# Feed forward as 2x2 blocks with seven multiplications, with the down part's right-hand blocks summed in the gate and up part and kept in DRAM

## The chip, the cores and the metric

The kernel runs on one core of one Trainium2 chip. The metric is the device time of one execution in microseconds; lower is better. The kernel before takes 1798.79 us, the median of 3 runs between 1797.85 and 1799.35.

## The reference

One layer of a decoder for one inference step: 1024 prompt tokens and 8 sample tokens (one each of 8 sequences with 2048 cached positions), 1024 channels, 8 heads, 2816 feed forward channels, all in fp32. What matters here is the end of the layer, cut from the reference:

```python
D_MODEL = 1024; SEQ = 1024; DEC_BATCH = 8; D_FF = 2816; N_HEADS = 8; D_V = 64

def _layer(x, c, pos, attend, ...):
    mod = jax.nn.silu(c) @ w_ada + b_ada
    sh1, sc1, gt1, sh2, sc2, gt2 = jnp.split(mod[:, None, :], 6, axis=-1)
    h = _rmsnorm(x, g_norm1) * (1 + sc1) + sh1
    ...
    o = attend(q_nope, q_pe, c_kv, k_pe)
    a = jnp.einsum("bshd,hde->bse", o, w_attn_o)
    ...
    m = jax.nn.sigmoid(gate_a) * a + jax.nn.sigmoid(gate_b) * bb
    x = x + gt1 * (m @ w_out)
    h2 = _rmsnorm(x, g_norm2) * (1 + sc2) + sh2
    gg, up = jnp.split(h2 @ w_gu, 2, axis=-1)
    x = x + gt2 * ((jax.nn.silu(gg) * up) @ w_down)
    return x, c_kv, k_pe, u_ext[:, -POOL_STATE:]
```

## The kernel before

Activations stand with channels on the 128 partitions and the T = 1032 tokens (8 sample tokens first, then the prompt) along the free axis. Each fp32 operand of a large product is split into a high and a low fp32r part: `split` (lines 97 and 106) makes the high part on ScalarE and the low part, source minus high part, on VectorE or GpSimd. `_mm3` (lines 71 to 73) then issues three matmuls for each 128 x 128 weight tile: high by high, high by low, low by high.

The layer runs in stages. First the input projection and the norms of queries, keys and values. Then the sample tokens' attention over the cached pages (`decode`) and the prompt's attention by heads (`attention`), between which a generator of fillers stands: projections of the gates and of the pooling branch, and `ada_unit` (line 142), which makes 128 of the 6144 gate coefficients `mod`. Units 16 to 47 are fillers. `back` follows. It loads the heads' outputs from DRAM, multiplies six of eight heads with `w_attn_o` while the last heads still run (`pm`, `wo_hi`, `wo_lo`; result in `part`), adds the last two heads' part (`rest`, with `wlh`, `wll`), applies the gates (`mt`, lines 1035 and 1044), multiplies with `w_out`, adds the residual (`gated_add`, line 999), sums squares by matmul (`st2`), and makes the second norm (`rstd2`, lines 1113 and 1114; multiply, line 1119). All this goes over three chunks of C3 = 344 tokens, and the weights of `w_out`, once split, stay in SBUF for all three.

`feed_forward` works in four parts of 6, 6, 5 and 5 tiles of 128 feed forward channels. A part makes gate and up for each of its tiles, eight k tiles in each of three chunks; silu, the product with up (line 1167) and the split follow. Then for each of the eight output tiles it multiplies the part's activations with `w_down` and adds the result to x1, which stays in SBUF. Weights come through `wload` (line 1138): a DMA from SyncE's queue, a split, and a slot of a ring of four pairs.

```python
for wh, wl in ws:
    acc = ps.tile([P, 512], F32, name="pj", tag="mm")[:, :C3]
    for k in range(8):
        _mm3(nc, acc, wh[:, k], wl[:, k], h2[i][0][k], h2[i][1][k], k == 0, k == 7)
    accs.append(acc)
```

The order on each engine comes from a scheduler that takes the program's order as priority and moves an instruction ahead where its inputs and buffers are free; `_Urgent` marks some weights' loads as first. Buffers come from pools, where the tag names the buffer that a tile takes over, and a tile waits until its tag's last reader is done.

## Time and profile before

| | before |
|---|---|
| median of 3 runs | 1798.79 us |
| span of the profiled execution | 1798.7 us |
| TensorE busy (matmuls / weight loads) | 97% / 91% |
| VectorE, ScalarE, GpSimd busy | 46%, 34%, 17% |
| feed forward, 1047.0 to the end | 751.7 us |
| attention's last two heads, mixing and output projection, 833 to 1047 | 214 us |

A busy share is the time in which the engine ran an instruction, over the span. Matmuls overlap, so a matmul's duration is longer than the distance to the next one, and the work done is read from counts and from first and last starts. The granted clock of TensorE is given as a share of full speed.

### The profile page before, as it was taken

Reading aid. Unit: us, or ns where it says so; the run is one execution under the profiler, and the core shown is the slowest. Engines: PE = TensorE matmul, PEld = TensorE weight load, DVE = VectorE, ACT = ScalarE, POOL = GpSimd, SP = SyncE. Lnnn points to the kernel's source line nnn. Section 1 sums busy time; section 2 is a strip of 40 time slices with the busy share of each in tenths; the row PEclk is TensorE's granted clock in tenths of the full one; section 3 lists DMA queues with packets and bytes.
Section 4 is the critical chain, followed back from the end, with each engine's and each line's share of the span. In section 5 each row is a group of like instructions: output and inputs, shape, how many; then the busy total and the mean of one; then the engine's idle time right before and its main releaser. Section 6 shows DMA issues by size and latency. Waiting matters only on the chain.

```text
span 1798.7 us, 30723 instructions
## 1 busy us (share of the span) xinstructions
PE 1741.1 (97%) x11840; PEld 1641.8 (91%) x11840; DVE 828.8 (46%) x1731; ACT 614.2 (34%) x1521; POOL 307.2 (17%) x336
## 2 busy tenths in 40 slices
PE   6799999999999999999989999999999999999999
PEld 5799999789687899998889899999999999999999
DVE  5656665547332455555787852233222322242223
ACT  5433555546341355545542332211221112111210
POOL 2524201001011223222575630000000000000000
PEclk9899999999999999999999999999999999999999
DMA  9213635445636433335523211111111121111112
GB/s 376 63 58 105 209 99 151 147 131 158 186 101 204 157 124 125 124 122 179 158 86 97 70 42 53 36 48 60 47 42 36 53 59 39 30 62 47 39 57 82
DMA packets 112147, 182.70 MB, mean 102 GB/s; under 512 B 15193, under 2 KB 86770, under 8 KB 110978
## 3 DMA queue, kind: packets, MB, share of 16 engines
q1 hardware_dynamic: 112002, 180.75, 32.4%
q8 instruction: 93, 1.52, 0.4%
q14 instruction: 52, 0.43, 0.1%
HBM read 151.77 MB, written 28.93 MB: 100 GB/s over the span
## 4 chain that ended last, share of the span: by engine, by line
PE 80%; DMA 4%; DVE 4%; issue 2%; ACT 1%; POOL 1%; SPq 1%; DVEq 0%; ACTq 0%; POOLq 0%
PE pj L71 19%; PE pj L72 19%; PE pj L73 19%; PE kn L71 4%; PE kn L72 3%; PE kn L73 3%; PE dacc L958 2%; PE tpp L679 2%; PE ada_ps L142 1%; PE av L693 1%; PE av L694 1%; PE sc L71 1%; PE sc L73 1%; PE sc L72 1%; PE tp L628 1%
## 5 line engine op out<-in xcount | busy, mean ns | idle before, releaser
L73 PE MATMUL pj<-h2h,fw 128*128 128x344 f32 x1056 | 337.1, 319 | 0.0
L72 PE MATMUL pj<-h2l,fw 128*128 128x344 f32 x1056 | 336.9, 319 | 0.0
L71 PE MATMUL pj<-h2h,fw 128*128 128x344 f32 x1056 | 335.7, 319 | 0.0
L73 PEld LDWEIGHTS pj<-h2h,fw 128*128 128x128 f32 x1056 | 198.3, 188 | 0.0
L72 PEld LDWEIGHTS pj<-h2l,fw 128*128 128x128 f32 x1056 | 198.2, 188 | 0.0
L71 PEld LDWEIGHTS pj<-h2h,fw 128*128 128x128 f32 x1056 | 198.1, 188 | 0.0
L97 ACT ACTIVATE fw<-fraw 128x1024 fp32r<-128x1024 f32 (+2 forms) x76 | 72.0, 948 | 302.4 <-PE pj L72 302.4
L73 PE MATMUL pj<-acth,fw 128*128 128x344 f32 x528 | 169.0, 320 | 0.0
L72 PE MATMUL pj<-actl,fw 128*128 128x344 f32 x528 | 168.9, 320 | 0.0
L71 PE MATMUL pj<-acth,fw 128*128 128x344 f32 x528 | 168.6, 319 | 0.0
L71 PE MATMUL pj<-hh,wt_hi 128*128 128x344 f32 x480 | 159.8, 333 | 0.0
L1167 DVE TENSOR_TENSOR silu<-silu,pj 128x344 f32<-128x344 f32 x66 | 33.8, 512 | 270.7 <-PE pj L73 270.7
L72 PE MATMUL pj<-hl,wt_hi 128*128 128x344 f32 x480 | 157.5, 328 | 0.0
L73 PE MATMUL pj<-hh,wt_lo 128*128 128x344 f32 x480 | 157.4, 328 | 0.0
L71 PE MATMUL kn<-wuh,lh 128*128 128x256 f32 (+1 forms) x512 | 150.4, 294 | 1.9 <-ACT nr L903 1.0
L72 PE MATMUL kn<-wul,lh 128*128 128x256 f32 (+1 forms) x512 | 145.3, 284 | 0.0
L73 PE MATMUL kn<-wuh,ll 128*128 128x256 f32 (+1 forms) x512 | 144.9, 284 | 0.0
L902 ACT ACTIVATE dsq<-kn 128x256 f32<-128x256 f32 x256 | 95.1, 380 | 111.5 <-PE kn L73 103.5
L999 DVE SCALAR_TENSOR_TENSOR x<-pj,mod,x 128x344 f32<-128x344 f32 (+1 forms) x96 | 55.0, 573 | 149.9 <-PE pj L73 149.9
L106 DVE TENSOR_TENSOR fw<-fraw,fw 128x1024 fp32r<-128x1024 f32 (+2 forms) x76 | 83.5, 1099 | 76.5 <-ACT fw L97 74.5
L904 DVE TENSOR_REDUCE ssq<-dsq 128x8 f32<-128x512 f32 x128 | 86.7, 679 | 52.5 <-ACT dsq L902 52.0
L71 PEld LDWEIGHTS kn<-wuh,lh 128*128 128x128 f32 x512 | 96.6, 189 | 13.0 <-issue 5.7
(328 smaller groups left out, 3778.9 us busy)
## 6 DMA issues: line engine op xcount, KB each, us to landing
fraw<-wgu_t SPq DMA_DIRECT2D x44, 512.0 KB, 3.6
pg<-cpack SPq DMA_DIRECT2D x128, 144.0 KB, 2.4
ln<-cnat SPq DMA_DIRECT2D x128, 128.5 KB, 2.4
wraw<-wada_t SPq DMA_DIRECT2D x32, 512.0 KB, 3.9
wraw<-win_t SPq DMA_DIRECT2D x20, 512.0 KB, 4.2
nat_d<-nat SPq DMA_DIRECT2D x8, 1024.0 KB, 4.5
natr<-nat_d SPq DMA_DIRECT2D x8, 1024.0 KB, 5.2
fraw<-wdn_t SPq DMA_DIRECT2D x16, 384.0 KB, 3.2
```

What stands on the lines that cost most here:

```text
L71: nc.tensor.matmul(out, sh, mh, start=first, stop=False)
L72: nc.tensor.matmul(out, sh, ml, start=False, stop=False)
L73: nc.tensor.matmul(out, sl, mh, start=False, stop=last)
L97: nc.scalar.activation(dst, src, AF.Copy)
L106: e.tensor_tensor(dl, src, dh.bitcast(F32), op=ALU.subtract)
L142: nc.tensor.matmul(acc[32 * j:32 * j + 32, 0:P], self.sT[:, kt, :], w[:, kt], start=(kt < 4), stop=(kt >= 4), tile_position=(0, 32 * j))
L679: nc.tensor.transpose(tp[:, s, i * P:(i + 1) * P], pn[:, i, kb * P:(kb + 1) * P], self.ident)
L902: nc.scalar.activation(sq[:, half].rearrange("p h d -> p (h d)"), kn[:, o:o + 256], AF.Square)
L904: nc.vector.tensor_reduce(ssq[:, j, t], sq.rearrange("p a h d -> p (a h) d"), axis=AX.X, op=ALU.add)
L958: nc.tensor.matmul(acc[32 * j:32 * j + 8, :W], p[:, j, t], ln[:, j], start=(t == 0), stop=False, tile_position=(0, 32 * j))
L999: nc.vector.scalar_tensor_tensor(dst[:, s0:], acc[:, s0:], gt[:, j, 8:9], res[:, s0:], op0=ALU.mult, op1=ALU.add)
L1167: nc.vector.tensor_tensor(s, s, accs[1], op=ALU.mult)
```

## The change

The feed forward's two products are each cut into 2 x 2 blocks and made with seven block products instead of eight (Winograd's form). The token columns are the two halves of 516 (`T2`). Each half is in turn handled as two pieces of `HC` = 258 columns, so a "half" `i` of the program, 0 or 1, holds one piece of both column blocks.

Gate and up: the left matrix has gate and up as its block rows, even and odd k tiles as its block columns; the right matrix is h2. In each of the 22 steps, `weights` loads gate and up weights of one tile and `left` makes four sums of their blocks on GpSimd (`sums`), then splits all seven left blocks (`wst`, tags w0 to w6). The seven right blocks (`cmb`) of each half are made once, in `norm`: four are sums of h2 blocks (`tcm`, lines 1131 to 1134, on VectorE and GpSimd). A step's products run over both halves, 12 matmuls of 258 columns each; PSUM holds running sums, which ScalarE copies out between products (`p1`, `u2`, `u4`), VectorE adds, and GpSimd multiplies with silu of the gate.

Down: the left matrix is w_down with output tiles 0 to 3 and 4 to 7 as block rows, even and odd feed forward tiles as block columns; the right matrix is the activations. After each second step VectorE makes the four sums of right blocks and both halves' seven blocks go to DRAM (`stg`, `cmb_d`, line 1316). Steps 1 to 12 also load parts of w_down, sum them on GpSimd (`dsum`) and write them to DRAM (`ws_d`). After step 22 the seven products follow one after the other, each over 11 k tiles, four output tiles and two halves: right blocks are loaded (`cml`, line 1369) and split, left blocks loaded (line 1378) and split into three rotating pairs of buffers. A product is added to x1, which goes through DRAM in between (`x1_d`; loaded again as `xacc`, line 1338), in `add`; the last two adds of an output tile write it out.

To make this fit, `back` goes over two halves of 516 columns in place of three chunks. The output weights are loaded and split for each half. For the second half the part of six heads is kept (`six`) while the first half's mixing runs with all eight heads. Eight of the 32 filler units of gate coefficients, 40 to 47 (`gt2`, which only the down part needs), move into step 0 of the feed forward (`gate_late`).

Cut to the core (comments and the new mixing code left out; the new lines are those of the changed kernel):

```diff
-FPARTS = (6, 6, 5, 5)
+T2 = T // 2
+HC = T // 4
...
-        units = iter(range(16, 48))
+        units = iter(range(16, 40))
...
+            def norm(i, x1, st, cm, tiles):
+                rs = xw.tile([P, T2], F32, name="rstd2", bufs=1)
+                nc.scalar.activation(two(rs), st, AF.Sqrt, scale=1.0 / DM, bias=self.eps)
+                nc.vector.reciprocal(rs, rs)
+                yield
...
+                    nc.vector.tensor_tensor(x, x, rs, op=ALU.mult)
...
+                    nc.scalar.activation(x, x, AF.Identity, scale=self.a2[:, j, 8:9], bias=sh2[:, j, 8:9])
...
+                for o in range(2):
+                    for q in range(4):
+                        act(2 * q + o)
+                        put(o, q, x1[2 * q + o][:, n1])
+                        yield
+                tm = tiles(i)
+                for r2 in range(2):
+                    for q in range(2):
+                        b11, b21 = x1[4 * r2 + 2 * q], x1[4 * r2 + 2 * q + 1]
+                        t1, t2, t3, t4 = (z[:, q * HC:(q + 1) * HC] for z in tm[r2])
+                        nc.vector.tensor_tensor(t1, b11[:, n2], b11[:, n1], op=ALU.subtract)
+                        nc.gpsimd.tensor_tensor(t3, b21[:, n2], b11[:, n2], op=ALU.subtract)
...
+    def sums(self, s, a11, a12, a21, a22):
+        tt = self.nc.gpsimd.tensor_tensor
+        tt(s[0], a21, a22, op=ALU.add)
+        tt(s[1], s[0], a11, op=ALU.subtract)
+        tt(s[2], a11, a21, op=ALU.subtract)
+        tt(s[3], a12, s[1], op=ALU.subtract)
+    def left(self, a11, a12, a21, a22, n):
...
+        for o, src in enumerate((a11, a12, s[1], s[2], s[0], s[3], a22)):
+            w = self.W.tile([P, 8, P], F32R, name="wst", tag=f"w{o}")
+            self.split(w[:, 0:n], w[:, 4:4 + n], src, "a")
...
+            for f in range(NF):
+                if f:
+                    w = weights(f)
...
+                for i in range(2):
+                    b[i] = bank("fb")[:, :HC]
+                    run(b[i], 0, i)
+                    p1[i] = t("p1")
+                    nc.scalar.activation(p1[i], b[i], AF.Copy)
...
+                for i in range(2):
+                    run(b[i], 4, i, True)
+                    u4[i] = t("u4")
+                    nc.scalar.activation(u4[i], b[i], AF.Copy)
+                    nc.vector.tensor_tensor(u4[i], d[i], u4[i], op=ALU.add)
+                for i in range(2):
+                    run(b[i], 5, i, True)
+                    nc.scalar.activation(n2[i], b[i], AF.Silu)
+                    nc.gpsimd.tensor_tensor(n2[i], n2[i], u4[i], op=ALU.mult)
...
+                        nc.sync.dma_start(self.cmb_d[:, f // 2, :, i].rearrange("o p n -> p o n"), z)
+                if f == 0:
+                    for k in range(40, 48):
+                        self.gate_late(k, ev, bank)
+                elif units:
...
+                    self.sums([s[:, k, :n] for k in range(4)], raws[0][:, 0:n], raws[0][:, 4:4 + n], raws[1][:, 0:n],
+                              raws[1][:, 4:4 + n])
...
+            x = xp.tile([P, T], F32, name="xacc", tag=f"xa{j}")
+            nc.sync.dma_start(x, self.x1_d[j])
...
+        for n, (o, s, blk, dm, h, new, final) in enumerate((
+                (0, None, (0, 0), 0, 0, True, False), (2, 1, None, 4, 0, False, False), (4, 0, None, 4, 1, False, False),
+                (5, 3, None, 0, 1, False, True), (1, None, (0, 1), 0, 0, True, True), (3, 2, None, 4, 1, True, True),
+                (6, None, (1, 1), 4, 0, False, True))):
+            for q in range(NP):
+                z = self.sp.tile([P, T2], F32, name="cml", tag=f"s{q % 4}")
+                nc.sync.dma_start(two(z), self.cmb_d[o, q])
...
+                for p0, k in ((0, 6), (6, 5)):
+                    raw = self.fw.tile([P, 8, P], F32, name="fraw")[:, :k]
...
+                    hl = [self.W.tile([P, 8, P], F32R, name="wdn", tag=f"w{(2 * nw + z) % 6}")[:, :k] for z in range(2)]
```

VectorE at the last norm, before: the third chunk's root is inverted, then multiplies with it (line 1119) alternate with the low parts of h2 (line 106) and with the activations of the first feed forward tile (silu).

```order
L1114 RECIPROCAL rstd_13179<-rstd_13179 128x344
L1167 TENSOR_TENSOR silu<-silu,pj 128x344
L1119 TENSOR_TENSOR t_13182<-x_2_12890,rstd_13179 128x344
L1119 TENSOR_TENSOR t_13189<-x_2_12890,rstd_13179 128x344
L106 TENSOR_TENSOR actl<-silu,acth 128x344
L106 TENSOR_TENSOR h2l<-t_13182,h2h 128x344
L1119 TENSOR_TENSOR t_13196<-x_2_12890,rstd_13179 128x344
L106 TENSOR_TENSOR h2l<-t_13189,h2h 128x344
```

The same engine now, at the norm of the second half (rstd, line 1104; x1b is x1 of that half):

```order
L1104 RECIPROCAL rstd_13324<-rstd_13324 128x516
L1109 TENSOR_TENSOR x1b<-x1b,rstd_13324 128x516 x8
L1131 TENSOR_TENSOR tcm<-x1b 128x258 x2
L109 TENSOR_TENSOR cmb<-x1b,cmb 128x258
L1131 TENSOR_TENSOR tcm<-x1b 128x258
L109 TENSOR_TENSOR cmb<-x1b,cmb 128x258
L1131 TENSOR_TENSOR tcm<-x1b 128x258
L1133 TENSOR_TENSOR tcm<-x1b,tcm 128x258
L109 TENSOR_TENSOR cmb<-x1b,cmb 128x258
```

Eight multiplies of 516 columns now stand in a row behind the reciprocal, and the first low part that the feed forward needs (cmb) stands behind them and two differences.

TensorE where the feed forward begins, before: the last output projection matmuls (pj from mh and wout) and the first of gate (fw0, fw1: weight tile, high and low part).

```order
L72 MATMUL pj_13143<-ml_12816,wout0_12317 128x344
L73 MATMUL pj_13143<-mh_12815,wout1_12318 128x344
L71 MATMUL pj_13260<-h2h_12381,fw0_13248 128x344
L72 MATMUL pj_13260<-h2l_12382,fw0_13248 128x344
L73 MATMUL pj_13260<-h2h_12381,fw1_13249 128x344
L71 MATMUL pj_13260<-h2h_12390,fw0_13248 128x344
```

TensorE now, at the end of the first product's first half and behind it (fb and fa: sums of the first and second product; wst_13303 and wst_13306: their weights; cmb_13263 is of the second half, the other cmb are of the first):

```order
L1255 MATMUL fb_13421<-cmb_12574,wst_13303 128x258
L1256 MATMUL fb_13421<-cmb_12576,wst_13303 128x258
L1257 MATMUL fb_13421<-cmb_12574,wst_13303 128x258
L1255 MATMUL fb_13436<-cmb_13263,wst_13303 128x258
L1255 MATMUL fa_13451<-cmb_12577,wst_13306 128x258
L1256 MATMUL fa_13451<-cmb_12579,wst_13306 128x258
L1257 MATMUL fa_13451<-cmb_12577,wst_13306 128x258
```

The matmuls of one tile followed one another; now a single matmul of the second half stands between the first half's first product and its second, in the place where the second half's first right block comes in.

SyncE's queue where the last gate and up tiles end, before: the fourth part's loads of gate and up weights, of down weights, then the outputs.

```order
L1138 DMA fraw<-wgu_t 128x1024 x10
L1138 DMA fraw<-wdn_t 128x640 x8
L1138 DMA fraw<-wgu_t 128x1024 x10
L1138 DMA fraw<-wdn_t 128x640 x6
L1178 DMA o_yT<-x_0_11920 128x344
```

SyncE's queue now, at the border between the gate and up part and the down part (stg: the last pair's blocks; fraw: left blocks; xacc: x1 back from DRAM, x_d; cml: right blocks):

```order
L1369 DMA cml<-cmb_d 128x516 x6
L1378 DMA fraw<-wdn_t 128x768
L1369 DMA cml<-cmb_d 128x516 x2
L1316 DMA cmb_d<-stg 128x7x258 x2
L1378 DMA fraw<-wdn_t 128x640
L1338 DMA xacc<-x_d 128x1032 x8
L1369 DMA cml<-cmb_d 128x516
L1378 DMA fraw<-ws_d 128x768
```

The last blocks' write stands ahead of eight loads of x1, and the load that reads these blocks back (the one cml behind xacc) stands behind them. On TensorE, 108 matmuls of the down part stand between the last of the gate and up part and the first that reads this load.

## Rows read from the trace of the kernel before

**Rows 1.** The page: busy time of each engine; granted clock in 40 slices.

```profile
PE 1741.1 (97%) x11840; PEld 1641.8 (91%) x11840; DVE 828.8 (46%) x1731; ACT 614.2 (34%) x1521; POOL 307.2 (17%) x336
...
PEclk9899999999999999999999999999999999999999
```

**Rows 2.** Windows: us, then busy us (count) of PE, PEld, DVE, ACT, POOL; clock, DMA share, GB/s.

```profile
833.00:1047.00 214.00, 196.64 (x1229) 185.25 (x1222) 165.89 (x352) 94.89 (x220) 117.75 (x111) 0.98 0.40 119
835.30:873.90 38.60, 31.37 (x184) 26.22 (x183) 28.64 (x83) 22.84 (x64) 13.62 (x16) 0.96 0.93 283
873.90:917.00 43.10, 43.10 (x300) 42.12 (x299) 33.01 (x92) 22.83 (x63) 23.65 (x26) 1.00 0.23 72
917.00:1047.00 130.00, 119.87 (x721) 114.94 (x720) 103.29 (x176) 46.91 (x85) 80.15 (x70) 0.97 0.29 86
1047.00:1798.70 751.70, 748.19 (x4760) 747.90 (x4758) 217.87 (x383) 134.74 (x217) 7.91 (x9) 1.00 0.16 48
```

**Rows 3.** Matmuls and weight loads by form: busy us, mean ns of one, idle before.

```profile
L73 PE MATMUL pj<-h2h,fw 128*128 128x344 f32 x1056 | 337.1, 319 | 0.0
...
L73 PEld LDWEIGHTS pj<-h2h,fw 128*128 128x128 f32 x1056 | 198.3, 188 | 0.0
...
L73 PE MATMUL pj<-acth,fw 128*128 128x344 f32 x528 | 169.0, 320 | 0.0
...
L71 PE MATMUL pj<-mh,wout 128*128 128x344 f32 x192 | 62.0, 324 | 0.0
...
L71 PE MATMUL pm<-o,wo_hi 128*128 128x344 f32 x72 | 24.5, 341 | 2.1 <-ACT o L97 2.0
...
L71 PE MATMUL pm<-o,wlh 128*128 128x344 f32 x24 | 9.0, 376 | 5.0 <-DVE mt L1035 4.6
```

**Rows 4.** Feed forward: one line's matmuls with first and last start; the last matmul.

```profile
L71 PE MATMUL pj<-h2h,fw x1056: 313/318/324, 1047.4 to 1737.8; 128*128 128x344 f32 x176
...
1794.87 0.32 PE L73 MATMUL pj<-acth,fw 128*128 128x344 f32 x1
```

**Rows 5.** Timeline of TensorE, matmuls of 256 and 264 columns: start, duration.

```profile
302.02 0.28 PE L71 MATMUL kn<-wuh,lh 128*128 128x256 f32 x1
...
302.73 0.32 PE L73 MATMUL pj<-hh,wt_lo 128*128 128x344 f32 x1
...
303.37 0.28 PE L71 MATMUL kn<-wuh,lh 128*128 128x264 f32 x1
...
304.11 0.32 PE L71 MATMUL pj<-hh,wt_hi 128*128 128x344 f32 x1
```

**Rows 6.** Element-wise work by form, VectorE, ScalarE and GpSimd.

```profile
L106 DVE TENSOR_TENSOR ll<-pg,lh 128x512 fp32r<-128x512 f32 x64 | 48.1, 754 | 48.2 <-ACT lh L97 46.6 <-DMA ln<-cnat 1.5
...
L97 ACT ACTIVATE lh<-pg 128x512 fp32r<-128x512 f32 x64 | 40.3, 630 | 30.6 <-PE kn L72 22.0 <-DMA pg<-cpack 8.2 <-DVE st L566 0.2
...
L106 DVE TENSOR_TENSOR actl<-silu,acth 128x344 fp32r<-128x344 f32 x66 | 33.9, 514 | 23.5 <-ACT acth L97 23.5
...
L1044 POOL TENSOR_TENSOR mt<-part,mt 128x344 f32<-128x344 f32 x24 | 27.1, 1147 | 3.4 <-DVE mt L1035 3.2 <-ACT wout L97 0.3
...
L1068 POOL TENSOR_TENSOR part<-part,mt 128x344 f32<-128x344 f32 x24 | 23.4, 977 | 26.7 <-DVE mt L1035 24.5 <-DVE mx L659 2.0
...
L106 DVE TENSOR_TENSOR ml<-mt,mh 128x344 fp32r<-128x344 f32 x24 | 22.8, 967 | 0.5 <-ACT mh L97 0.5
```

**Rows 7.** Tile rstd, last norm: duration ns min/median/max, first and last start.

```profile
L1113 ACT ACTIVATE rstd<-st,eps x3: 547/549/550, 979.9 to 1053.7; 128x344 f32<-128x344 f32 x3
L1114 DVE RECIPROCAL rstd<-rstd x3: 2303/2303/2303, 980.5 to 1054.3; 128x344 f32<-128x344 f32 x3
```

**Rows 8.** DMA issues with median us to landing; a window of heavy loading.

```profile
fraw<-wgu_t SPq DMA_DIRECT2D x44, 512.0 KB, 3.6
...
o_d<-ot SPq DMA_DIRECT2D x32, 64.0 KB, 2.8
...
20.00:45.00 25.00, 24.39 (x304) 21.16 (x303) 17.43 (x29) 11.83 (x20) 11.06 (x14) 1.00 1.00 396
```

**Rows 9.** Matmuls of the gate coefficients, by form.

```profile
L142 PE MATMUL ada_ps<-wraw,sT 128*32 128x128 f32 x512 | 30.6, 281 | 0.0
```

More of the change, by code (lines that the diff above doesn't have):

```diff
@@ L1075, in back @@
             for j in range(8):
[L1076 to L1081 removed]
+                raw, w = wo(j, 4)
+                acc = ps.tile([P, 2, 512], F32, name="pj", tag="mm")[:, :, :HC]
+                for h in range(2):
+                    cs = slice(h * HC, (h + 1) * HC)
+                    for k in range(4):
+                        _mm3(nc, acc[:, h], w[0][:, k], w[1][:, k], os[0][k][0][:, cs], os[0][k][1][:, cs], k == 0,
+                             k == 3)
@@ L1088, in back @@
                 for j in range(8):
+                    raw = fw.tile([P, 8, P], F32, name="fraw")
+                    nc.sync.dma_start(raw, I["wout_t"][j])
+                    wh, wlo = (self.W.tile([P, 8, P], F32R, name="wout", tag=f"w{3 + 2 * (j % 2) + n}") for n in range(2))
+                    self.split(wh, wlo, raw, "a", WOE[j])
                     if i == 0:
-                        raw = fw.tile([P, 8, P], F32, name="fraw")
-                        nc.sync.dma_start(raw, I["wout_t"][j])
@@ L1109, in back @@
+                    nc.scalar.activation(sq, x, AF.Square)
+                    if j == 7:
+                        sqs.append(sq)
+                    else:
+                        sqs.append([xw.tile([P, T2], F32R, name=z, tag=z) for z in ("sqh", "sql")])
+                        self.split(*sqs[j], sq, "a")
                     if j:
                         stat(j - 1)
+                    for _ in range(3):
+                        next(todo, None)
                 stat(7)
-                rs = xw.tile([P, C3], F32, name="rstd2", bufs=1)
@@ new lines, in back, with combos @@
+                for _ in todo:
+                    pass
+                self.comb.append(self.combos(i))
+                todo = norm(i, x1, st, self.comb[i], temps)
+            first = weights(0)
+            for _ in todo:
+                pass
+        self.feed_forward(c, gt2, weights, first)
+    def combos(self, i):
+        return [[[self.m(f"c{i}_{14 * r + 2 * o + hl}", "cmb", F32R).rearrange("p (q n) -> p q n", q=2)
+                  for r in range(2)] for hl in range(2)] for o in range(7)]
@@ L1182, in _tables, with gate_late @@
+    def gate_late(self, i, pool, bank):
+        nc = self.nc
+        w = self.fw.tile([P, 8, P], F32, name="fraw")
+        nc.sync.dma_start(w, self.I["wada_t"][i])
+        acc = bank("ada_ps")
+        for kt in range(8):
+            j = kt % 4
+            nc.tensor.matmul(acc[32 * j:32 * j + 32, 0:P], self.sT[:, kt, :], w[:, kt], start=(kt < 4), stop=(kt >= 4),
+                             tile_position=(0, 32 * j))
+        self.ada_sum(i, pool, acc, None, None)
 def _tables():
```

390 lines of the change are left out of this document (238 added, 152 removed).

## Prediction

> **What bounds the kernel now.** Read the page's busy times and the granted clock first [rows 1]: TensorE is busy 97% of the span, at its upper level of 2.4 GHz nearly throughout. The profiled execution spans 1798.7 us, the median of the runs is 1798.79, so a sum against the span holds for the median. Next the windows [rows 2]: from 1047 us to the end stands the feed forward, 751.7 us with TensorE busy 748.2, VectorE 217.9, ScalarE 134.7, GpSimd 7.9. Only fewer or cheaper matmul slots shorten that stretch, and three engines have room. The 214 us before it (last two heads, mixing, output projection) hold 196.6 us of TensorE, with real holes.
>
> How many slots: the gate and up groups have 1056 matmuls on each of three lines and the down groups 528 [rows 3], together 4752 of 344 columns. The first starts at 1047.4, the last at 1794.87 [rows 4]: 747.5 / 4751 = 157.3 ns each. The 319 ns of [rows 3] is latency, pipelined two deep; a reader who multiplies by it gets twice the stretch.
>
> **What a matmul of 258 columns takes.** Six of 256 columns lie between 302.02 and 302.73, six of 264 between 303.37 and 304.11 [rows 5]: 118.3 and 123.3 ns. The line from 256 to 344 columns has (157.3 - 118.3) / 88 = 0.443 ns a column, so 119.2 ns at 258; I take 119, with 118 and 123 as ends. The line leaves only some 5 ns that don't shrink with the columns.
> By the Trainium skill, TensorE: Matmul & The Clock Gate, section Back-to-back issue gap, sustained matmuls in real kernels cost 81 ns at 128 columns and 131 at 512, so halves are dear. An estimate by it has 98 ns at 258 and 109 at 344, 25 us more for the new feed forward instead of 88 less. The trace disagrees: 39 ns between 256 and 344 columns where that rule gives 11.
>
> **The sum, feed forward.** Gate and up: 22 steps x 7 products x 4 x 3 x 2 halves = 3696 matmuls; down: 7 x 4 x 2 x 11 x 3 = 1848. 5544 x 0.119 = 659.7 us against 747.5: **-87.8**. Columns fall by exactly an eighth; nearly all of it arrives. Given back:
>
> 1. Norm of the second half. Before, the last chunk's norm ran while TensorE already worked on two ready chunks. Now there is one ready half, and the order on VectorE puts eight 516-wide multiplies first. Chain from the last output-projection matmul: gated add and square 0.75 + 0.64 [rows 6], four statistics slots about 0.5, square root 0.55 x 1.5 = 0.8 and reciprocal 2.30 x 1.5 = 3.45 [rows 7], eight multiplies x 0.75 = 6.0 (754 ns for 512 elements, [rows 6]), two differences and a low part at 0.4 each: 13.4 us. TensorE has 24 matmuls (2.9 us) to put in. The low parts then drip in, some 3 us more. Stall **13**; 8 if multiplies cost as the 514 ns row scaled, 20 if they are stretched like the 967 ns one.
> 2. Eight units of gate coefficients move here. 512 such matmuls took 30.6 us [rows 9], 64 take **3.8**; 0 if they fall into the stall. Their weight tiles are those of step 1: load 3.6 us [rows 8], three GpSimd sums and a split, 9.4 us against 72 matmuls (8.6) on hand: **3** with the start of the splits, 0 to 8. Taken out of the attention they give back about 4 there.
> 3. The border to the down part. The last pair's combinations need an add, two GpSimd products, a difference (2.3 us), the writes to DRAM (two of 0.92 MB, 4.7 at the 396 GB/s of [rows 8]), then stand on SP's queue behind eight loads of x1, 4.2 MB at the same rate = 10.7, then their own load 3.2 (512 KB took 3.6, [rows 8]) and split 0.6: 21.5 us. The order shows 108 down matmuls ahead, 12.9 us. Stall **9**; 0 if the loads don't queue, 15 if the writes wait too.
> 4. Steady steps: per step (20.0 us of TensorE) ScalarE has seven hi parts x 0.63 and ten small reads x 0.4 = 8.4; VectorE seven low parts x 0.75, six adds x 0.4 and half of eight differences: 9.3; GpSimd four sums of 512 x 1.45 (977 / 344 ns an element, [rows 6]), four products x 0.73, and in steps 1 to 12 up to four more sums: 14.5. All fit below 20, with weights prepared a step ahead, so they cost nothing; a cover gone is rival 2. I allow 0.2 us a step, **4** (0 to 11).
> 5. Down: per product 31.4 us of TensorE, VectorE about 19. Three weight pairs rotate, so the second part of the next column tile has 33 matmuls (3.9 us) for a split of about 1.9: **2** (0 to 14). Loads of 5.7 MB per product need 181 GB/s of the 396 seen.
> 6. Tail after the last matmul: 1794.87 to 1798.7, 3.8, the same.
>
> 659.7 + 13 + 3.8 + 3 + 9 + 4 + 2 + 3.8 = 698.3 against 751.3 from 1047.4 on: **-53**.
>
> **The sum, before the feed forward.** Matmul slots hardly change: 288 of 344 columns for w_attn_o (72 and 24 a line, [rows 3]), 576 for w_out [rows 3] and 48 statistics give 143.5 us; now 384 + 768 + 56 of 258 give 143.8. Output weights are split twice (16 x 1024 elements), on engines with room. What moves is when: about 138 instead of 210 filler matmuls lie beside heads 6 and 7. These took 38.6 and 43.1 us; in the second TensorE was busy throughout, in the first the DMA queue 93% [rows 2], with loads that now come later. I take 33 and 34 (-14.7): TensorE alone would allow 26 and 32 (31.4 - 54 x 0.157 + 24 x 0.119 and 43.1 - 156 x 0.157 + 114 x 0.119), and the head's own chain of exponent, transpose and split may hold all 81.7. What is put off comes after: 1058 matmuls x 0.119 = 126, plus 8 idle for the round trip of the last heads through DRAM (a write of 2.8 us [rows 8], a load, two splits) and 4 at the lower clock, against 130.0 [rows 2]: +8. The moved units: -4 before. Rounded to **-8**, ends -26 and +12 (nothing gained in the heads, that stage as late again).
>
> 1798.7 - 53 - 8 = **1738 us**.
>
> **Rivals.**
> 1. Every cover holds: heads by TensorE alone, no queue at the border. -18 - 9: **1711**. For it: TensorE was busy all through head 7. Against: head 6 with little filler still took 38.6 us. Chance 0.18.
> 2. VectorE and GpSimd block each other in steps 1 to 12. For it: the same kind of VectorE subtract took 514 ns where GpSimd was quiet and 967 where it was busy [rows 6]. If all operations with two SBUF inputs took turns, a step would need 14.5 + 5.3 + 1.6 = 21.4 us, 23.8 with the PSUM reads between; at 22.3 it is 12 x 2.3 = +28: **1766**. Against: GpSimd's prices already come from a contended stretch. Chance 0.17. By the Trainium skill, SBUF — State Buffer, section Who interferes with whom, the port that VectorE and GpSimd share is held by one for a whole instruction, the loser blocked; the two rows agree in kind, none shows two full loads on it.
> 3. Slower: the ring of raw weights. In steps 1 to 12 the next raw tiles may load only after the last split of this step, which waits for its last products. From there: split 1.4, load 3.6, three sums, four more and four products (12.6 of GpSimd), split 1.4 = 19 us, and 24.3 until the third run needs it. Beyond 1.42 times the GpSimd row it decides; at twice the row a step grows by 7.3, 12 x 7.3 = +88: **1826**. For it: VectorE's row did nearly double. Against: GpSimd's own rows run only from 977 to 1147 ns there [rows 6]. It must reach about 1.8 times before the kernel is slower than now. Chance 0.06.
> 4. The change doesn't pay at all: a cost that every matmul has whatever its columns, its weight load of 188 ns [rows 3], of which now 792 more are issued. At 135 ns a matmul the whole -87.8 is gone: 1738 + 5544 x 0.016 = **1827**. Against: the 256-column matmuls carry the same load and keep 118 ns. Chance 0.03. (The rule weighed above points this way.)
>
> **How the numbers follow.** Forecast 0.56, rivals 0.18, 0.17, 0.06, 0.03. The forecast's own ends, with the terms not all bad at once, are 1718 to 1762. The range **1705 to 1775** adds rivals 1 and 2 nearly whole and leaves out 3, 4 and the far edges, under 0.2. Within 0.2% (3.6 us) counts as no change, about what a measurement of this kernel can tell apart. Forecast and rivals 1 and 2 are faster, 3 and 4 slower: faster 0.90, same 0.01, slower 0.09.
>
> **What would show it.** In the changed profile: matmuls of 258 columns at 119 ns in the steady steps, 20 us a step; a hole of TensorE of about 13 us after the output projection, ended by VectorE's low parts; one of about 9 at the border, ended by the load of the combinations or its split; GpSimd 14 us a step at most; the feed forward some 698 us long, starting about 8 us earlier. The prediction is wrong if steps last over 21 us with TensorE waiting for GpSimd or VectorE, if a 258-column matmul stands above 123 ns, or if the stretch before grows by more than 12.

## Result and profile after

The changed kernel takes 1820.69 us (median of 4 runs, 1815.3 to 1823.6) against 1799.07 (4 runs, 1797.9 to 1801.4) for the kernel before, a ratio of 1.0115 with a 95% interval of 1.0095 to 1.0135: 1.2% slower, where 1738 us was forecast. The profiled execution spans 1821.8 us.

First the page: busy times, and the granted clock in 40 slices (those of the kernel before are [rows 1]).

```profile
PE 1688.4 (93%) x12936; PEld 1586.4 (87%) x12936; DVE 1014.5 (56%) x1947; ACT 773.5 (42%) x1875; POOL 527.5 (29%) x501
...
PEclk9899999999999999999999989899999999989999
```

TensorE has 53 us less to do, and the span is 23 us longer: it has idle time now, 133 us of the span where it had 58. The windows of the changed kernel show where (columns as in [rows 2]): the last head but one and the last, then mixing, the output projection of the first half and of the second, the feed forward, and inside it step 1, a steady step and the step after it. Steps are counted from 1 from here on: step 1 is the program's f = 0, which the section on the change calls step 0.

```profile
832.70:861.80 29.10, 24.83 (x163) 21.75 (x162) 21.50 (x67) 20.77 (x58) 8.21 (x10) 0.94 0.24 73
861.80:901.20 39.40, 36.63 (x273) 33.38 (x271) 26.89 (x77) 27.57 (x77) 7.11 (x9) 1.00 0.42 124
...
901.20:934.30 33.10, 26.15 (x177) 25.14 (x178) 20.64 (x25) 12.34 (x20) 12.01 (x7) 0.79 0.71 232
934.30:993.70 59.40, 57.90 (x478) 57.40 (x477) 44.76 (x67) 23.08 (x32) 25.41 (x14) 1.00 0.55 159
993.70:1061.05 67.35, 54.46 (x423) 52.85 (x421) 52.65 (x84) 36.49 (x61) 26.57 (x17) 0.95 0.42 130
1061.05:1821.80 760.75, 699.00 (x5688) 690.91 (x5688) 398.99 (x634) 265.44 (x537) 265.97 (x228) 0.96 0.50 155
1061.05:1107.70 46.65, 34.14 (x313) 30.28 (x313) 27.42 (x54) 21.59 (x49) 15.38 (x12) 0.89 0.23 77
1159.50:1179.70 20.20, 20.20 (x170) 20.20 (x169) 10.95 (x16) 7.68 (x17) 13.67 (x11) 1.00 0.47 157
1179.70:1205.40 25.70, 21.95 (x170) 21.74 (x169) 11.95 (x20) 7.45 (x17) 13.27 (x12) 0.93 0.59 183
```

The feed forward starts 13.7 us later than before (1061.05 against 1047.4) and lasts 760.75 us, 9 longer. A steady step is what the forecast had, 168 matmuls in 20.20 us or 120.2 ns each, and the later down products take 31.70 us. So 22 x 20.20 + 7 x 31.70 = 666.3 us of the 760.75 are matmuls one behind the other, 81 us less than before; the other 94 are lost: 26.4 in step 1, 43.5 in steps 2 to 21 (their lengths less 20 x 20.20), 21.2 in step 22 and the first down product, 3.3 behind the last matmul. The profiled execution is the slowest of the four. Five of the kernels below (e2_border, e3_norm0, e4_norm1, e7_wov, e9_direct) leave the steps as they are, and their profiles lose 37.0 to 39.5 us in steps 2 to 21, so some 4 to 6 of the 43.5 belong to this one execution.

**The steps.** Lengths alternate: steps 3, 5, 7, ... last 21 to 30 us, most of the even ones 20.2. Steps 2 to 21 as one window; the waits of VectorE and TensorE in the steps (us in all, number, longest); and the chain in one of the long ones (timeline of the changed kernel, step 13; in brackets the idle time before the instruction and what ended it):

```profile
1107.69:1555.16 447.47, 419.66 (x3361) 416.69 (x3361) 236.09 (x342) 153.42 (x346) 244.63 (x209) 0.96 0.47 146
...
DVE stg L1288 <- DMA cmb_d<-stg: 66.3, 20, 6.9
...
PE fb L1255 <- ACT u L1300: 26.3, 12, 5.9
...
1376.34 0.43 DVE L1288 TENSOR_TENSOR stg<-fa,p 128x258 f32<-128x258 f32 x1 [5.62 <-DMA cmb_d<-stg]
1376.80 0.42 ACT L1296 ACTIVATE stg<-stg 128x258 f32<-128x258 f32 x1 [4.32 <-DVE stg L1288]
...
1379.35 0.43 DVE L1288 TENSOR_TENSOR stg<-fa,p 128x258 f32<-128x258 f32 x1 [1.98 <-DMA cmb_d<-stg]
...
1379.81 0.42 ACT L1296 ACTIVATE stg<-stg 128x258 f32<-128x258 f32 x1 [2.07 <-DVE stg L1288]
1380.14 0.64 ACT L1300 ACTIVATE u<-fb 128x258 f32<-128x258 f32 x2
...
1380.56 0.57 PE L1255 MATMUL fb<-cmb,wst 128*128 128x258 f32 x1 [1.89 <-ACT u L1300]
```

Line 1288 adds the gate's sum into the staging tile `stg`, of which there is one for each half. Every second step it may write only when the DMA of the pair before has read the tile (line 1316). Behind the add, ScalarE's silu waits (line 1296), behind the silu the copy `u` out of PSUM (line 1300), and TensorE may not add into that bank before the copy. The same happens for each half; the second half's chain, from 1379.35 on, is the one that ends TensorE's 1.89 us. In steps 2 to 21 TensorE stands idle for 27.8 us (447.47 less 419.66 busy). The other 15.7 of the 43.5 are matmuls further apart than 120.2 ns, at a mean granted clock of 0.96.

**The border.** Timeline of SyncE's queue, VectorE, ScalarE and TensorE between the two parts:

```profile
1585.74 0.98 SPq L1316 DMA_DIRECT2D cmb_d<-stg  x2
...
1594.61 3.79 SPq L1338 DMA_DIRECT2D xacc<-x_d  x8
1594.70 0.11 DVE L1341 MEMSET smp<- 128x64 f32 x1 [7.92 <-DMA cmb_d<-stg]
...
1598.44 0.46 SPq L1369 DMA_DIRECT2D cml<-cmb_d  x1
...
1608.05 0.63 ACT L100 ACTIVATE bh<-cml 128x516 fp32r<-128x516 f32 x1 [17.12 <-DMA cml<-cmb_d]
...
1608.73 1.01 PE L1255 MATMUL fc<-bh,wdn 128*128 128x258 f32 x3 [17.09 <-ACT bh L100]
```

The loads of x1 go into memory of the staging tiles, and so does the memset, which waited for the last write; the loads left only when that write was done, 3 us after TensorE's last matmul (1591.6). The load of the last block stands behind them: one hole of 17 us.

### The profile page after: what moved, and what is told of

Same layout as the page of the kernel before. It is cut to its first block, busy times and chain, and to the rows that moved or that the text cites. A ratio compares the mean times of both kernels' runs of the same rounds, so it can differ in the third digit from the quotient of the medians.

```text
span 1821.8 us, 34407 instructions
## 1 busy us (share of the span) xinstructions
PE 1688.4 (93%) x12936; PEld 1586.4 (87%) x12936; DVE 1014.5 (56%) x1947; ACT 773.5 (42%) x1875; POOL 527.5 (29%) x501
## 5 line engine op out<-in xcount | busy, mean ns | idle before, releaser
L1255 PE MATMUL fb<-cmb,wst 128*128 128x258 f32 x704 | 207.9, 295 | 35.8 <-ACT u L1300 26.3
L1256 PE MATMUL fb<-cmb,wst 128*128 128x258 f32 x704 | 205.6, 292 | 0.7 <-DVE cmb L109 0.7
L1257 PE MATMUL fb<-cmb,wst 128*128 128x258 f32 x704 | 204.6, 291 | 0.0
L1255 PE MATMUL fc<-bh,wdn 128*128 128x258 f32 x616 | 174.4, 285 | 17.1 <-ACT bh L100 17.1
L1255 PEld LDWEIGHTS fb<-cmb,wst 128*128 128x128 f32 x704 | 139.7, 198 | 40.6 <-ACT u L1300 29.2
L1256 PE MATMUL fc<-bl,wdn 128*128 128x258 f32 x616 | 174.6, 284 | 0.0
L1257 PE MATMUL fc<-bh,wdn 128*128 128x258 f32 x616 | 173.1, 283 | 0.0
L1256 PEld LDWEIGHTS fb<-cmb,wst 128*128 128x128 f32 x704 | 139.7, 198 | 1.4 <-DVE cmb L109 1.4
L1257 PEld LDWEIGHTS fb<-cmb,wst 128*128 128x128 f32 x704 | 139.1, 198 | 0.0
L109 DVE TENSOR_TENSOR wst<-scm,wst 128x512 fp32r<-128x512 f32 x88 | 81.0, 922 | 93.2 <-ACT wst L100 91.7
L1255 PEld LDWEIGHTS fc<-bh,wdn 128*128 128x128 f32 x616 | 116.8, 190 | 17.5 <-ACT bh L100 17.3
L1256 PEld LDWEIGHTS fc<-bl,wdn 128*128 128x128 f32 x616 | 117.4, 191 | 0.0
L1257 PEld LDWEIGHTS fc<-bh,wdn 128*128 128x128 f32 x616 | 116.3, 190 | 0.3 <-DVE wdn L109 0.3
```

The costliest lines, as they stand in the source:

```text
L109: e.tensor_tensor(dl, src, dh.bitcast(F32), op=ALU.subtract)
L1255: nc.tensor.matmul(acc, sh, mh, start=first and not more, stop=False, **kw)
L1256: nc.tensor.matmul(acc, sh, ml, start=False, stop=False, **kw)
L1257: nc.tensor.matmul(acc, sl, mh, start=False, stop=last, **kw)
```

## The experiments

Times are medians; a kernel that was run once has its single time. The ratio is to the kernel before on the same chip.

| run | us | ratio, 95% interval |
|---|---|---|
| changed kernel | 1820.69 | 1.0115 [1.0095, 1.0135] |
| e1_own_tile | 1807.73 | 1.0038 [1.0025, 1.0051] |
| e5_vprod (e1 and VectorE products) | 1783.87 | 0.9917 [0.9894, 0.9940] |
| e6_nosum (e1 without the sums) | 1785.7 | one execution |
| e2_border | 1811.88 | 1.0056 [1.0037, 1.0075] |
| e9_direct | 1802.92 | 1.0014 [1.0001, 1.0026] |
| e3_norm0 | 1821.56 | 1.0110 [1.0092, 1.0127] |
| e7_wov | 1815.40 | 1.0090 [1.0068, 1.0113] |
| e4_norm1 | 1820.76 | 1.0115 [1.0095, 1.0134] |
| e11_all (e5, e7, e9) | 1762.42 | 0.9781 [0.9765, 0.9798] |
| e12_nonorm1 | 1748.4 | one execution |
| e13_spread | 1757.57 | 0.9757 [0.9742, 0.9772] |
| e14_halves | 1770.7 | one execution |
| e16_early | 1757.71 | 0.9754 [0.9738, 0.9771] |
| e17_nonorm0 | 1758.8 | one execution |
| e18_best | 1754.91 | 0.9745 [0.9732, 0.9759] |

**The steps: e1_own_tile, e5_vprod, e6_nosum.** The first takes the wait for the staging tile away:

```diff
-                    n1, n2 = [z[:, 0] for z in st], b12
+                    n1, n2 = [t(f"g{i}") for i in range(2)], b12
...
-                    nc.gpsimd.tensor_tensor(n1[i], n1[i], u2[i], op=ALU.mult)
+                    nc.gpsimd.tensor_tensor(st[i][:, f % 2], n1[i], u2[i], op=ALU.mult)
```

> The activated tile of every even-numbered step (f = 0, 2, ...) gets a buffer of its own until its last product; only that product writes into the block staging tile. Theory (the first add of every second step stands on VectorE behind the DRAM write of the pair before, and ScalarE's silu and the copies behind it hold TensorE): the long steps, 3 to 21, fall from a mean of 24.2 us to 20.2, the clock in them rises, and the time falls by 35 to 45 us, to about 1781 us. Rival (VectorE and GpSimd slow each other in the steps with sums): the long steps stay above 23 us and the time changes by under 5 us.

13 us came, not 35 to 45. Steps 13 to 21 are 20.20 us each, so there the theory holds. In steps 3 to 12 the holes moved: 22.7 us in the mean, now in other steps. Two windows of e1_own_tile, steps 10 and 15; waits of GpSimd, VectorE and TensorE (those of TensorE over all steps, the others from step 2 into step 12); and, in step 10, GpSimd's order and what VectorE waited for:

```profile
1287.80:1315.00 27.20, 22.23 (x170) 22.02 (x169) 11.74 (x16) 7.33 (x17) 16.62 (x16) 0.87 0.50 167
1400.20:1420.40 20.20, 20.20 (x171) 20.20 (x170) 11.01 (x20) 7.57 (x17) 8.20 (x8) 1.00 0.51 145
...
POOL dsum L1231 <- DMA fraw<-wdn_t: 28.2, 5, 6.8
POOL scm L1233 <- DMA fraw<-wgu_t: 22.5, 5, 7.1
...
DVE stg L1312 <- POOL stg L1309: 23.9, 4, 7.7
...
PE fb L1255 <- ACT u L1292: 17.4, 7, 5.0
...
1291.41 1.29 POOL L1233 TENSOR_TENSOR scm<-fraw 128x512 f32<-128x512 f32 x1 [3.27 <-DMA fraw<-wgu_t]
1292.66 1.28 POOL L1231 TENSOR_TENSOR scm<-fraw 128x512 f32<-128x512 f32 x1
1293.90 0.74 POOL L1305 TENSOR_TENSOR b<-b,u 128x258 f32<-128x258 f32 x1
...
1297.78 1.44 POOL L1309 TENSOR_TENSOR stg<-g,u 128x258 f32<-128x258 f32 x2
...
1298.56 0.95 DVE L1312 TENSOR_TENSOR stg<-b,stg 128x258 f32<-128x258 f32 x1 [7.65 <-POOL stg L1309]
```

GpSimd is not full (16.6 of 27.2 us). But the products that end a step (lines 1305 and 1309) stand in its order behind sums that wait for their raw tiles: in step 10 it stood idle 3.27 us for a tile, then made four sums (5.1 us) and line 1305's two products before line 1309. VectorE's differences wait for the products, the next step's add stands behind the differences, and TensorE waits again for a copy on ScalarE. Two runs test that. One moves the products, the other leaves the sums out:

```diff
-                    nc.gpsimd.tensor_tensor(n2[i], n2[i], u4[i], op=ALU.mult)
+                    nc.vector.tensor_tensor(n2[i], n2[i], u4[i], op=ALU.mult)
...
-                    nc.gpsimd.tensor_tensor(st[i][:, f % 2], n1[i], u2[i], op=ALU.mult)
+                    nc.vector.tensor_tensor(st[i][:, f % 2], n1[i], u2[i], op=ALU.mult)
```

> As e1_own_tile, and the four products of a step (silu times up and its like) go from GpSimd to VectorE. Theory (in steps 3 to 12 these products stand in GpSimd's order behind the down part's sums, which wait for their loads, and VectorE, ScalarE and TensorE wait for the products in turn): steps 3 to 12 of e1_own_tile, 22.7 us in the mean, fall to 20.2 to 20.8, the time by some 20 us to about 1788 us. Rival (the two engines slow each other, or the weights' split is late): steps 3 to 12 stay above 22 us.

> As e1_own_tile, with the sums of down weights on GpSimd left out: the loads and the writes to DRAM stay, and the first down part's left blocks are raw blocks in place of sums. Theory (the sums and their place in GpSimd's order make the holes in steps 3 to 12): these steps fall to 20.2 us, the span by about 20 us. Rival (the added loads and writes on SyncE's queue and the ring of raw tiles make them late): the holes in steps 3 to 12 stay.

Both did what the theory says: steps 3 to 21 last 20.2 to 20.5 us in both. In e5_vprod no wait of TensorE is left in steps 3 to 22; this is step 10, with one line on VectorE before and after GpSimd starts:

```profile
1270.20:1290.40 20.20, 20.20 (x170) 20.20 (x170) 17.48 (x20) 7.45 (x17) 14.16 (x10) 1.00 0.65 219
...
1271.07 0.43 DVE L1309 TENSOR_TENSOR stg<-g,u 128x258 f32<-128x258 f32 x1
...
1272.32 1.28 POOL L1233 TENSOR_TENSOR scm<-fraw 128x512 f32<-128x512 f32 x1 [2.50 <-DVE u L1308]
...
1274.08 1.51 DVE L1309 TENSOR_TENSOR stg<-g,u 128x258 f32<-128x258 f32 x1
```

VectorE and GpSimd are fuller here than in any step of the changed kernel shown above, 17.5 and 14.2 of 20.2 us, and VectorE is slower while GpSimd works: line 1309's product takes 0.43 us before GpSimd starts and 1.51 beside it. TensorE loses nothing by it, so this is not what made the holes. What both edits take away is the product behind a sum in GpSimd's order. Both also take work from GpSimd; that it stood idle for 10.6 of the 27.2 us of e1_own_tile's step 10 speaks against the load itself.

**The border: e2_border, e9_direct.** The first queues the block's load ahead of x1 and moves the memset; the second also takes the last block of the first product from SBUF:

```diff
-            nc.sync.dma_start(x, self.x1_d[j])
...
-        nc.vector.memset(smp, 0.0)
+        nc.gpsimd.memset(smp, 0.0)
...
+            if n == 0:
+                for j in range(8):
+                    nc.sync.dma_start(xs[j], self.x1_d[j])
```

```diff
+            direct = [self.m(tags[20 + k], "bd", F32R) for k in range(2)]
+            for i in range(2):
+                cs = slice(i * HC, (i + 1) * HC)
+                self.split(direct[0][:, cs], direct[1][:, cs], st[i][:, 0], "a")
```

> At the border to the down part the load of the last right block is queued ahead of the eight loads of x1, and the small memset that waits for the same memory goes from VectorE to GpSimd. Theory (the block's load waits for eight loads of x1): the hole of 17.4 us at the border falls to 6 to 9 us, the time by about 10 us, to 1811 us. Rival (the DRAM write itself is what lasts): the hole stays above 14 us and the time changes by under 3 us.

> As e2_border, and the last right block of the first down product is split straight from the staging tile, without the way through DRAM. Theory (the border is the round trip of the last blocks through DRAM, write, wait and load): the hole falls from 17.4 us in the changed kernel to under 3, the time to about 1802 us. Rival (the x1 loads or the weights' split hold the border): a hole of 6 us or more stays.

Both theories came true: the hole fell to 6.7 us and then went; 8.8 and 17.8 us came. TensorE's longest wait at the border, in the changed kernel, e2_border and e9_direct:

```profile
PE fc L1255 <- ACT bh L100: 17.1, 1, 17.1
```

```profile
PE fc L1255 <- ACT bh L100: 6.7, 1, 6.7
```

```profile
PE fb L1255 <- ACT u L1300: 0.7, 1, 0.7
```

So 10 of the 17 us were the queue behind x1, the rest the write and its way back. (e2_border moves the memset as well. In the changed kernel the chain to TensorE runs from the load over ScalarE, not over the memset's VectorE.)

**The stretch ahead: e3_norm0, e7_wov, e17_nonorm0.** In the changed kernel the second half's output projection takes 67.35 us for 423 matmuls (50.8 at 120.2 ns), while VectorE is busy 52.65 and ScalarE 36.49.

```diff
+                    y = nc.vector.tensor_tensor(x, x, rs, op=ALU.mult)
+                    after(y) if i == 0 else None
```

(`after` makes the scheduler keep the instruction behind the latest addition of the second half on VectorE.)

> The reciprocal and the multiplies of the first half's norm may no longer stand on VectorE ahead of the additions of the second half's output projection. Theory (this burst of 10 us holds the addition for which TensorE's next sum of squares waits): the hole of 6.5 us at 1008 us and the low clock behind it go, the stretch from the last head to the feed forward falls from 160 us to about 150, the time to about 1811 us. Rival (the second half's own mixing or weights hold TensorE there): a hole of the same size stays and the time changes by under 3 us.

A miss: the hole at 1008 us went, one of 11 opened at 1032, and the time stayed (timeline of e3_norm0):

```profile
1043.72 0.58 PE L72 MATMUL pj<-mh,wout 128*128 128x258 f32 x1 [10.99 <-POOL wout L109]
```

```diff
-                    self.split(wh, wlo, raw, "a", WOE[j])
+                    self.split(wh, wlo, raw, "a", "v" if i else WOE[j])
```

> As e3_norm0 (the first half's norm not ahead of the second half's additions), and the low parts of the output weights of the second half go to VectorE, none to GpSimd. Theory (in e3_norm0 the hole of 11.3 us at 1032 us waits for a low part on GpSimd, which is behind the norm's differences and the first step's weight sums): the hole goes, the stretch from the last head to the feed forward falls from 160 to about 148 us, the time to about 1810 us. Rival (VectorE, ScalarE and GpSimd simply have too much to do beside the second half's output projection): the hole only moves, the stretch stays above 156 us.

5.3 us came. The intervals of the two times overlap, so the time alone would not show it; the stretch does, 154.3 us against 159.9 (and 157.6 in e11_all, which has the same edit). It lies between the two. Leaving out the first half's norm decides it:

> As e11_all, with the first half's norm left out: its right blocks are those of the second half, so VectorE, ScalarE and GpSimd have nothing of it to do beside the second half's output projection; step 1 then waits for the second half's norm with all its products, so only the time up to the feed forward is read. Theory (the first half's norm, which my sum left out, takes these engines from the second half's output projection): the second half's projection and sums, 63 to 67 us in the runs so far for 420 matmuls (50.4 us at 0.12), fall to 51 to 55 us. Rival (the second half's weight splits and mixing alone are too much): it stays above 60 us.

Windows of the second half's projection up to the feed forward in e11_all, and up to its last sum of squares in e17_nonorm0 (there the feed forward then waits 7 us for the only norm):

```profile
996.70:1059.84 63.14, 54.97 (x422) 52.42 (x420) 50.89 (x88) 36.51 (x61) 22.09 (x13) 0.93 0.46 143
```

```profile
994.90:1047.60 52.70, 51.47 (x422) 50.97 (x420) 26.78 (x34) 21.46 (x31) 6.81 (x5) 1.00 0.52 159
```

Without that norm the projection runs at 125 ns a matmul. The norm costs it some 10 us even with both edits. In the changed kernel it would be some 14 (67.35 - 52.70, less 0.8 for the wait behind the last sum of squares), if the edits of e7_wov matter only with the norm there; no run leaves out the norm alone.

**Step 1: e4_norm1, e11_all, e12_nonorm1, e14_halves, e16_early, e13_spread.** e4_norm1 cuts the second half's reciprocal and multiplies in two, writes their order out and takes the differences from GpSimd:

```diff
+                    chain(nc.vector.reciprocal(rs[:, n1], rs[:, n1]))
+                    for o in range(2):
+                        for q in range(4):
+                            part(2 * q + o, n1)
+                            self.hi("a", cm[o][0][q // 2][:, q % 2], x1[2 * q + o][:, n1])
+                            if o:
+                                low(0, q)
```

> The norm of the second half is made for the first column block first (reciprocal, multiplies, low parts alternating on VectorE), and all its differences on VectorE, none on GpSimd. Theory (VectorE's eight wide multiplies ahead of the first low part, and GpSimd's slowed differences, hold TensorE in step 1): step 1 falls from 46.6 us to 36 to 40, the time to about 1813 us. Rival (step 1 waits for weights or the moved units of gate coefficients): step 1 stays above 44 us and the time changes by under 3 us.

A miss for the theory: step 1 took 47.5 us, as long as the rival has it. The first hole got shorter and a later one longer. TensorE's longest waits for the norm in step 1, in the changed kernel and in e4_norm1:

```profile
PE fb L1255 <- ACT cmb L100: 4.3, 1, 4.3
PE fd L1255 <- ACT cmb L100: 2.4, 1, 2.4
```

```profile
PE fd L1287 <- ACT cmb L100: 5.8, 1, 5.8
PE fb L1287 <- ACT cmb L100: 2.0, 1, 2.0
```

The run changes two things at once: with the order it puts the eight differences of 258 columns that GpSimd had on VectorE, 0.42 us each. VectorE's stretch in the norm is 24.5 us in both. The other runs start from e11_all:

> The edits of e5_vprod, e7_wov and e9_direct together. If the causes add up: 36.8 us (e5_vprod), 17.8 (e9_direct) and 5.3 (e7_wov) off 1820.7, to about 1761 us, and only step 1 stays long, at 46 to 48 us. If the causes share the same waiting time: 1768 us or more.

It adds up: 1820.7 - 36.8 - 17.8 - 5.3 = 1760.8, measured 1762.4. (The four executions of e5_vprod lie 9 us apart, so the parts are not known as well as the sum agrees.) e12_nonorm1 leaves out the second half's norm:

```diff
+            self.comb[1] = self.comb[0]
```

> As e11_all, with the second half's norm left out: its right blocks are those of the first half, so nothing of step 1 waits for it. Theory (step 1 is long because of the norm and of the low clock that follows its holes): step 1 falls from some 47 us to 24 to 26 (20.2, the moved units of gate coefficients and a start). Rival (the moved units and the weights behind them hold it): step 1 stays above 32 us.

33.1 us, where e11_all has 48.5: by its words the rival's, just above 32, so something besides the norm lengthens step 1. But the norm is the larger part: 15.4 us went, of which step 3 took back 4.4, and over the whole feed forward the norm's hold is worth 11.7 us (700.4 against 688.7). e14_halves runs all seven products of the first half first:

```diff
+                stages = (s0, s1, s2, s3, s4, s5, s6)
+                for g, i in ([(g, i) for i in range(2) for g in stages] if f == 0 else
+                             [(g, i) for g in stages for i in range(2)]):
+                    g(i)
```

> As e11_all, with the first step's seven products run for the first half before any of the second half. Theory one (TensorE's order alone keeps it from using the first half's 84 matmuls while the norm runs): step 1 falls to 34 to 40 us. Theory two (the first half's sums can't be copied out before the norm ends, since their buffers lie in memory that the norm still uses, so the third product waits): step 1 stays above 43 us or grows.

```profile
PE fb L1263 <- ACT p L1298: 19.1, 1, 19.1
...
1082.57 0.39 ACT L1298 ACTIVATE p<-fb 128x258 f32<-128x258 f32 x1 [3.07 <-DVE cmb L109]
```

Theory two: step 1 grew to 52.5 us, with one wait of TensorE for the copy `p`. Its buffer is in a pool laid over the norm's tiles, and ScalarE wrote it only when the norm's last low part (cmb) was done on VectorE. With memory of its own the copies run between the norm's instructions:

```diff
+        self.ep = c.enter_context(tc.tile_pool(name="ep", bufs=1))
...
-                    p1[i] = t("p1")
+                    p1[i] = self.ep.tile([P, HC], F32, name="p1e") if f + i == 0 else t("p1")
```

> As e14_halves, with buffers of their own for the first half's three copies of step 1 in memory that the norm does not use, and with the second half's norm in the order of e4_norm1. Theory two of e14_halves: the first half's seven products, 10 us, run beside the norm, step 1 falls to 32 to 38 us, the time some 10 us below e11_all. Rival (ScalarE and VectorE are full with the norm, so the copies come late all the same): step 1 stays above 43 us.

Step 1 fell to 39.7 us, step 2 rose from 22.4 to 27.2; 4.7 us net, half of what was expected. The order of e4_norm1 came with the buffers, so what each is worth by itself stays open. e13_spread moves the units:

```diff
-                if f == 0:
-                    for k in range(40, 48):
-                        self.gate_late(k, ev, bank)
-                elif units:
+                if 13 <= f < 21:
+                    self.gate_late(27 + f, ev, bank)
+                if f and units:
```

> As e11_all, with the eight moved units of gate coefficients taken out of step 1 and put one each into steps 14 to 21. Theory (with the norm left out step 1 still took 33.1 us in e12_nonorm1, 12.9 more than a steady step: the units' matmuls and the late weights of step 2, which share raw buffers with the units): step 1 falls by 6 to 10 us, steps 14 to 21 grow by 0.5 us each, the time falls by 3 to 6 us from that of e11_all, 1762.4. Rival (the units fill time in which TensorE waits anyway): step 1 falls by under 3 us, the time stays or grows by up to 3 us.

Steps 1 and 2 fell by 10.8 us, and each step with a unit grew by 1.0 us, not 0.5, so the feed forward gained 1.5 us (700.4 to 698.9). The rest of the 4.9 us between the medians lies ahead of it, where the edit changes nothing, and the two intervals overlap. The units cost 8 to 11 us wherever they stand. e18_best joins the two:

> As e16_early, with the units spread as in e13_spread. If both gains stand: 1757.7 less 3 to 6, about 1753 us. If the units only filled holes: 1757 to 1761 us.

1754.9 us, 2.55% faster than the kernel before: 2.8 below e16_early, at the edge of the first case, with intervals that overlap. Its feed forward lasts 694 us, step 1 29.9:

```profile
1056.90:1751.00 694.10, 681.86 (x5688) 677.43 (x5688) 451.47 (x739) 266.09 (x546) 188.99 (x133) 0.99 0.54 169
1056.90:1086.80 29.90, 25.19 (x169) 24.35 (x170) 27.12 (x61) 20.02 (x44) 7.95 (x2) 0.85 0.01 1
```

## Why the prediction was wrong, point by point

- **A matmul of 258 columns: right.** 120.2 ns against 119, inside 118 to 123. The -87.8 became -81. By the Trainium skill, TensorE: Matmul & The Clock Gate, section Back-to-back issue gap, a sustained matmul costs 81 ns at 128 columns and 131 at 512. The 20.20 us step disagrees, as [rows 5] did: 120.2 ns at 258 columns and 157.3 at 344 lie 37 apart, where the prediction's estimate from the page has 11. Rival 4 falls by the 120.2 ns, where it needs 135.
- **Steady steps, 4 us with ends 0 and 11: the step that failed most.** Measured 43.5. "All fit below 20 ... so they cost nothing" added up each engine's busy time, and that sum was about right (ScalarE 7.7, VectorE 11, GpSimd 13.7 in a step with all sums). It asked how much each engine has to do, never what each instruction waits for. The staging tile's write stood in the diff, with one buffer a half, and an add two products into the next pair that overwrites it. The sum charged the write only at the border. e1_own_tile shows this wait; e5_vprod and e6_nosum show the second behind it, GpSimd's products queued behind sums whose loads come late. Some 16 of the 43.5 are the lower clock that follows the holes, which the sum had here at nothing too. By the Trainium skill, PSUM — Partial Sum Buffer, section Engine vs sequencer instructions, the queues of ScalarE, VectorE and GpSimd are strictly first in, first out; the timeline of step 13 agrees: TensorE had ended the sum in `fb` at 1378.7, and ScalarE copied it out only at 1380.14, behind a silu that waited for VectorE's add.
- **Rivals 2 and 3** put a price on GpSimd's load and on the ring of raw tiles. Rival 3 had the late raw tiles right, but what they held up was the step's own products, not the next weights. Rival 2 is right that one engine slows the other (0.43 and 1.51 us above) and wrong on the price: in e5_vprod both engines are busier than in the changed kernel's steady step, and its steps last 20.2 us.
- **The border, 9 and 2 us: too small.** 21.2 measured, 17.1 of it the one hole. The queue behind x1 was named, priced about right (14.1 us from the loads' start at 1594.61 to the end of the block's split, against 10.7 + 3.2 + 0.6) and is shown (e2_border). The cover of 108 matmuls was there too. What was too small is what stands ahead of the loads: the write of the last pair's blocks started 7.0 us after the last matmul of the gate and up part (1578.7 to 1585.74) instead of 2.3, with VectorE splitting down weights and right blocks between the pair's sums, and the two writes took 8.9 us instead of 4.7. The sum had the loads start when the write ends, as they do; it did not say that this is because they take over the staging tile's memory.
- **Norm of the second half, 13 us: right in size by luck, wrong in mechanism.** e12_nonorm1 puts it at 11.7 us over the feed forward. But there is no hole of 13 us ended by VectorE's first low parts: the longest is 4.3, ended by ScalarE's high part, and more follow. Nor does the order of the multiplies, on which the sum built, set it alone: e4_norm1 changed it, with the differences moved as well, and step 1 stayed. The norm takes VectorE 24.5 us in both, and the first half's later products could not fill the time because their copies had no memory (e14_halves; e16_early gave them some).
- **The moved units, 3.8 and 3 us: too small.** 10.8 us in steps 1 and 2, 1.0 us each in later steps. Only the eight matmuls of a unit were priced; the sums behind them and their waits were not. Step 1 in all: 26.4 lost against 19.8.
- **Before the feed forward, -8: wrong sign, +13.7.** The terms given for it, -14.7, +8 and -4, add up to -10.7; -8 is not their sum. The heads' end moved about as far as expected: from the 917.0 us at which the sum cut its window to 901.2, 15.8 us where 18.7 were expected. (The last head's last matmul itself ended at 922.9 before; 5.9 us of that head lie in the sum's next stage.) Mixing lost about 12 us of waiting and low clock in 33.1 us, as the sum had. The second half's output projection lost 16.6 of 67.35 us, and the sum had nothing there: it priced the norm of the second half and forgot that of the first, which now runs beside the other half's projection. e17_nonorm0 shows that it is this norm. A stretch that grows by more than 12 was one of the prediction's own signs of being wrong, and so were steps over 21 us with TensorE held by GpSimd or VectorE; both came (TensorE waited for ScalarE, which waited for VectorE).

The balance against 1738: 39.5 from the steps, 21.7 from the stretch ahead, 10.2 from the border, 6.6 from step 1, 6.6 from 120.2 instead of 119 ns, less 0.5 in the tail: 84.1, against 1821.8 - 1738 = 83.8.

What stays open: of the hold ahead of the feed forward, the 10 us that e11_all still loses to the first half's norm; nothing was tried that shortens the norm itself. How much of the products' delay on GpSimd is the late loads and how much the sums' own time is not separated by any run; step 10 of e1_own_tile shows both, 3.27 us idle for a load and 5.1 us of sums.

## What to carry to other kernels

Where every engine has room in its busy time, list for each instruction in a loop what it must wait for, DMA reads of a buffer that it overwrites among them, and what stands behind it on the same in-order engine; here the loop ran at TensorE's pace, 20.2 us a step, only when none of these waits reached it. When a transformation saves matmuls by adding sums on other engines, keep the step's own products off the queue on which those sums wait for their loads. At a border between stages look at which new buffers lie over old ones: the wait is not in the code's dataflow, and it had a part in two of the holes here, at the x1 loads and at the first step's copies.

## What the runs showed that was not expected

- One GpSimd subtraction of 258 columns lasted 6.45 us where the median was 0.96, while VectorE ran one instruction behind the other (source line 1132 of the changed kernel; min, median and max in ns). In e14_halves the same subtraction lasts 6.46 us. Why is not shown.

```profile
L1132 POOL TENSOR_TENSOR tcm<-x1b x4: 722/958/6448, 1069.5 to 1078.0; 128x258 f32<-128x258 f32 x4
```

- Holes are paid twice, in idle time and in the clock behind them. From 1080 to 1090 us the mean granted clock was 0.68, between TensorE's two levels of 1.2 and 2.4 GHz, after 20 us in which it was busy 4.9 and 6.8 us of each 10; 46.65 us of step 1 at a mean of 0.89 are at most some 5 us, an estimate (46.65 x 0.11). In step 5, too, the clock is 0.93 where it is 1.00 in step 4.

```profile
1060.00:1070.00 10.00, 4.93 (x27) 4.37 (x25) 8.94 (x12) 5.52 (x10) 0.48 (x1) 0.83 0.22 63
1070.00:1080.00 10.00, 6.82 (x70) 5.47 (x68) 8.03 (x19) 7.26 (x17) 10.00 (x6) 1.00 0.06 19
1080.00:1090.00 10.00, 6.58 (x29) 5.88 (x30) 6.34 (x11) 5.21 (x12) 1.93 (x3) 0.68 0.24 88
```
